# Seven half products in place of eight for the second MLP's first product, with the residual spilled there too

## The chip, the cores and the metric

The kernel runs on one core of a Trainium2 chip. The metric is the device time of one execution in microseconds (us); lower is better. Five engines work side by side, each on its own instruction queue: TensorE (PE in the profile; its weight loads are PEld), VectorE (DVE), ScalarE (ACT), GpSimd (POOL) and SyncE (SP), which here issues the DMAs.

## The reference

Two layers over 512 latent tokens and 256 context tokens with 1024 channels. Layer 0 mixes tokens by pooling, layer 1 by attention; each is followed by a squared-ReLU MLP with 4096 inner channels. In the second layer only the latent tokens go through the MLP.

```python
def sq_relu_mlp(h, w_in, w_out):
    return jnp.square(jax.nn.relu(h @ w_in)) @ w_out
...
        x = x + gt1 * rms_norm(y_lat, g_mix_post[i])
        m_lat = sq_relu_mlp(modulate(rms_norm(x, g_mlp_pre[i]), sh2, sc2), w_mlp_in[i], w_mlp_out[i])
        x = x + gt2 * rms_norm(m_lat, g_mlp_post[i])
```

Everything is float32. `h @ w_in` is called the first product below, the product with `w_out` the second.

## The kernel before

Each float32 operand of a product is kept as two parts, a high part rounded to the matmul's number format and a low part that holds the rest; a product is three matmuls, high x high, high x low, low x high. ScalarE makes the high part (a copy), VectorE the low part (a subtraction). This is what `split` (line 120 ff.) and `Ring.load` (line 129 by its helper) do with every weight tile that a DMA brings into one of three raw buffers.

An MLP (`mlp`) runs over 16 groups of 256 inner channels. For each group it loads 256 columns of `w_in` and 256 rows of `w_out`, computes the first product and its squared ReLU into `hid`, and then the second product for each tile of 128 tokens (`out_mm`, line 748), which `out_ev` (lines 757 to 761) adds to the accumulator `acc`. The second product of group g comes behind the first product of group g + 1. The last two groups' second products are put together, and the closing steps `last0` or `last1` (norm, gate, residual) are woven between their tiles.

The first MLP (layer 0, 768 tokens) and the second (layer 1, 512 tokens) differ in the first product.

- The second MLP uses `Inner` for all its groups: two blocks of 128 inner channels, each 8 slices of 128 channels times 3 parts, so 48 matmuls of 128 x 512 (line 535). `square` takes ReLU and square of each block. Its weights go through `ring1`, four buffers used in turn, two for `w_in` and two for `w_out`.
- The first MLP uses `Inner` for groups 0 and 1 only and `Seven` for groups 2 to 15. There tokens, channels and inner channels are each cut in half, and of the eight half products seven are computed, from sums of halves (the scheme of Strassen in Winograd's form): `chain` is one half product, 4 slices x 3 parts = 12 matmuls, here 384 tokens wide (line 648), and `run` chains the seven through four PSUM banks `a`, `b`, `c`, `e`. Between the products ScalarE copies a partial sum from bank to bank (lines 656 to 662) and VectorE folds two of them into SBUF (lines 664, 666).

Once per MLP `sums` computes the four sums of activation halves (S1 to S4, lines 593 to 596) from the float32 activations, which still lie in `acc`, the place of the second product's sum. The room for S1 to S4 is that of the residual `xr`, the gate and a scratch tile: the residual is written to DRAM (`spill`, line 572), the pool is closed, and another is opened in its place. For each group `weights_sums` computes the sums of weight halves (T1 to T4) and splits them (lines 614 to 631); their only place is `unit[1]` and the now unused quarter of the activations. The second product's weights have one place, `unit[2]`, refilled in two halves (lines 120, 121). Before the last stage `before0` closes the sums' pool, builds the gate anew (`gate_diag`, lines 305 to 311) and reads the residual back (line 1013).

In the second MLP the residual and the gate stay where they are. `extra1` computes the last gate's modulation on VectorE in four of the groups (`ada_sum`, lines 254 to 263) and its gate at group 10.

PSUM is used as two tiles of two banks (`psA`, for the first product) and four tiles of one bank (`psB`, for the second product, transposes and gates). The order of the instructions on each engine is made when the kernel is built: the framework's scheduler takes the program's order and moves instructions by simulated times (`schedule_with_timeline_sim=True`), some of them pinned with `keep_in_program_order`. So matmuls of the second product lie between those of the first.

Of the kernel before, what the change touches and what calls it, by code (L numbers as in the profile page):

```python
# [9 lines left out]
F32 = mybir.dt.float32  # L10
# [7 lines left out]
P = 128  # L18
D = 1024
KT = D // P  # L20
LAT = 512
# [32 lines left out]
def backbone(ctx: ExitStack, tc, x, c, ctx_in, c_ctx, w_ada, b_ada, g_mix_pre, g_mix_post,  # L54
# [11 lines left out]
    held = ExitStack()  # L66
# [6 lines left out]
    xr, gate, junk = residents(held)  # L73
# [489 lines left out]
    place_of = [(t % 2) * 3 + t // 2 for t in range(NT)]  # L563

    HN = TOK // 2
    quad = lambda z, u, h: [z[:, 4 * u + k, HN * h:HN * h + HN] for k in range(4)]
    A11, A12, A21, A22 = ((quad(hH, u, h), quad(hL, u, h)) for h in range(2) for u in range(2))
    S = {}

    def sums():  # L570
        for t in (4, 5, 0, 1, 2, 3):
            sy.dma_start(spill[:, t], xr[:, t])
        held.close()
        S["held"] = ExitStack()
        pool = S["held"].enter_context(tc.tile_pool(name="sums", bufs=1, side="right"))
        f, parts[0] = pool.tile([P, 8520], F32R, name="sums"), pool.tile([P, 192], F32, name="parts")
        u = unit[0]
        n4 = 4 * HN
        at = {1: (f[:, 0:n4], f[:, n4:2 * n4]), 2: (f[:, 2 * n4:3 * n4], f[:, 3 * n4:4 * n4]),
              4: (u[:, 0:n4], u[:, n4:2 * n4])}  # L580
        k4 = lambda z: [z[:, HN * k:HN * k + HN] for k in range(z.shape[-1] // HN)]
        for n, (hi, lo) in at.items():
            S[n] = k4(hi), k4(lo)
        h3, l3 = f[:, 4 * n4:5 * n4], [u[:, 2 * n4:2 * n4 + 2 * HN], f[:, 5 * n4:5 * n4 + 2 * HN]]
        S[3] = k4(h3), [z for x in l3 for z in k4(x)]
        src = acc.rearrange("p (q u k h n) -> p u h k q n", u=2, k=4, h=2, n=P)

        def put(n, j, a, b, op):
            hs = slice(2 * HN * j, 2 * HN * j + 2 * HN)
            wide = lambda z: z.rearrange("p (k q n) -> p k q n", k=2, n=P)  # L590
            w = work_tile()[:, 0:2 * HN]
            for m in range(2):
                ve.tensor_tensor(out=wide(w)[:, m], in0=a[:, m], in1=b[:, m], op=op)
            hi, lo = (h3[:, hs], l3[j]) if n == 3 else (z[:, hs] for z in at[n])
            sc.copy(hi, w)
            ve.tensor_tensor(out=lo, in0=w, in1=hi, op=ALU.subtract)
            return wide(w)

        for j in range(2):
            a11, a21, a12, a22 = (src[:, u, h, 2 * j:2 * j + 2] for u in range(2) for h in range(2))  # L600
            w1 = put(1, j, a21, a22, ALU.add)
            w2 = put(2, j, w1, a11, ALU.subtract)
            put(4, j, a12, w2, ALU.subtract)
            put(3, j, a11, a21, ALU.subtract)

    def weights_sums(g):
        raw = raw_load(w_mlp_in[0, :, g * 256:(g + 1) * 256].rearrange("(k p) n -> p k n", p=P), 256)
        rv = raw.rearrange("p (k h n) -> p h k n", h=2, n=P)
        b11, b12, b21, b22 = (rv[:, h, 4 * u:4 * u + 4] for u in range(2) for h in range(2))
        k4 = lambda z: z.rearrange("p (k n) -> p k n", n=P)  # L610

        def put(reg, src, n):
            hi, lo = reg[:, 0:n], reg[:, n:2 * n]
            sc.copy(k4(hi), src)  # L614
            ve.tensor_tensor(out=k4(lo), in0=src, in1=k4(hi), op=ALU.subtract)
            ops = lambda z: [[z[:, 512 * m + P * k:512 * m + P * k + P] for k in range(4)] for m in range(n // 512)]
            return list(zip(ops(hi), ops(lo)))

        B11, B21 = put(unit[1][:, 0:2048], rv[:, 0], 1024)
        tt = work_tile()  # L620
        t1, t2 = k4(tt[:, 0:512]), k4(tt[:, 512:1024])
        ve.tensor_tensor(out=t1, in0=b12, in1=b11, op=ALU.subtract)
        ve.tensor_tensor(out=t2, in0=b22, in1=t1, op=ALU.subtract)
        T1, T2 = put(unit[1][:, 2048:4096], k4(tt), 1024)
        tu = work_tile()
        ve.tensor_tensor(out=k4(tu[:, 0:512]), in0=b22, in1=b12, op=ALU.subtract)
        ve.tensor_tensor(out=k4(tu[:, 512:1024]), in0=b21, in1=t2, op=ALU.subtract)
        def put3(m0, nm, src):
            hi, lo = (z[:, 0:4, HN + P * m0:HN + P * (m0 + nm)].rearrange("p k (m n) -> p m k n", n=P) for z in (hH, hL))
            sc.copy(hi, src)  # L630
# [621 lines left out]
```

## Time and profile before

| | |
|---|---|
| time, median of 3 runs | 1220.46 us (1219.82 to 1220.71) |
| the profiled execution | 1220.63 us, its span 1218.7 us |
| TensorE busy | 1172.3 us, 96% of the span |
| VectorE busy | 903.3 us, 74% |
| ScalarE busy | 566.6 us, 46% |
| first MLP's groups 2 to 15 | about 150 to 580 us of the span |
| second MLP | from 852 us, steady from 916 us; last stage from 1190 us |

A row of a group of instructions gives line, engine, operation, output <- inputs, shape and count, then busy us and mean ns of one, then the idle time of the engine before them and what ended it. In the chain of waits a row gives start, length and what ran; the chain steps of a run of matmuls give their pace, since a single matmul's own duration (390 ns at 512 wide) overlaps its neighbours'. A busy TensorE is not one at its peak.

### The profile page before, as it was taken

How to read it: one execution, taken by the hardware profiler on the slowest of the kernel's cores; microseconds unless marked ns; L12 is line 12 of the kernel's file. 1: busy time of each engine (PE TensorE's matmuls, PEld its weight loads, DVE VectorE, ACT ScalarE, POOL GpSimd, SP SyncE). 2: the span in 40 equal slices, each digit the busy share in tenths (PEclk: the TensorE clock that was granted, in tenths of full speed). 3: DMA queues.
4: the chain of work that ended last, by engine and by line, in shares of the span. 5: the costliest groups of instructions: out<-in, count | busy, mean ns of one | idle time of the engine just before them, and what ended most of it. 6: DMA issues, size and time to landing. Idle time of an engine off the chain costs nothing.

```text
span 1218.7 us, 16348 instructions
## 1 busy us (share of the span) xinstructions
PE 1172.3 (96%) x6434; PEld 1016.1 (83%) x6434; DVE 903.3 (74%) x1494; ACT 566.6 (46%) x969; POOL 103.5 (8%) x135
## 2 busy tenths in 40 slices
PE   6799999999999999999989989999899999999997
PEld 5579899998899889988878879988778888888886
DVE  3888968889899979876777689853566775546555
ACT  5676445443355345445575468844442312223222
POOL 1061000000000000000451231001000000000001
PEclk9999999999999999999999989999999999999999
DMA  9994024444344344423323011030244443322301
GB/s 327 348 341 160 6 99 139 138 138 157 120 139 138 118 159 134 143 104 117 126 69 104 35 35 36 1 105 1 70 138 138 138 138 108 134 70 70 104 1 69
DMA packets 105003, 143.67 MB, mean 118 GB/s; under 512 B 2608, under 2 KB 88032, under 8 KB 104928
## 3 DMA queue, kind: packets, MB, share of 16 engines
q1 hardware_dynamic: 104928, 142.64, 35.3%
q8 instruction: 50, 0.82, 0.3%
q14 instruction: 25, 0.20, 0.1%
HBM read 137.39 MB, written 5.24 MB: 117 GB/s over the span
## 4 chain that ended last, share of the span: by engine, by line
PE 41%; DVE 3%; issue 3%; ACT 2%; POOL 2%; POOLq 0%; DVEq 0%; ACTq 0%
PE pso L748 14%; PE psin L535 14%; PE psy L1115 3%; PE po L1089 3%; PE pss L1050 2%; PE psq L876 2%; PE pspt L1075 1%; ACT junk L154 1%; DVE xr L319 1%; POOL rs L885 1%; DVE work L901 0%; POOL ms L165 0%; POOL rs L167 0%; PE psx L344 0%; DVE units L1078 0%
## 5 line engine op out<-in xcount | busy, mean ns | idle before, releaser
L748 PE MATMUL pso<-units,rb 128*128 128x512 f32 x1542 | 369.8, 391 | 2.3 <-DVE units L129 1.2
L748 PEld LDWEIGHTS pso<-units,rb 128*128 128x128 f32 x1542 | 288.1, 188 | 60.0 <-ACT units L120 1.9
L761 DVE TENSOR_TENSOR acc<-acc,pso 128x512 f32<-128x512 f32 x239 | 155.4, 681 | 91.4 <-PE pso L748 91.0
L259 DVE SCALAR_TENSOR_TENSOR rows<-raw,cond,rows 128x256 f32<-128x256 f32 x280 | 124.5, 483 | 1.0
L748 PE MATMUL pso<-ra,rb 128*128 128x512 f32 (+1 forms) x390 | 91.3, 386 | 0.0
L165 POOL TENSOR_SCALAR ms<-ss 128x1 f32<-128x1 f32 x21 | 11.1, 527 | 942.9 <-ACT junk L154 942.2
L535 PE MATMUL psin<-ra,units 128*128 128x512 f32 (+1 forms) x320 | 87.5, 373 | 0.1
L748 PEld LDWEIGHTS pso<-ra,rb 128*128 128x128 f32 x390 | 72.5, 188 | 15.1 <-ACT rb L550 0.4
L126 ACT CAST units<-raw 128x2048 fp32r<-128x2048 f32 (+1 forms) x29 | 40.3, 1417 | 93.6 <-PE pso L748 76.5
L535 PE MATMUL psin<-ra 128*128 128x512 f32 x256 | 80.5, 390 | 0.0
L126 ACT CAST ra<-raw 128x2048 fp32r<-128x2048 f32 x16 | 30.4, 1907 | 96.2 <-PE pso L748 68.4
L648 PE MATMUL psin<-ra,units 128*128 128x384 f32 x336 | 66.1, 339 | 0.7 <-ACT psin L660 0.6
L535 PEld LDWEIGHTS psin<-ra,units 128*128 128x128 f32 x320 | 58.6, 188 | 9.1 <-ACT work L544 0.3
L648 PE MATMUL psin<-sums,units 128*128 128x384 f32 x336 | 64.4, 339 | 1.5 <-ACT units L614 1.4
L648 PEld LDWEIGHTS psin<-ra,units 128*128 128x128 f32 x336 | 59.4, 188 | 4.2 <-ACT psin L660 0.9
L648 PEld LDWEIGHTS psin<-sums,units 128*128 128x128 f32 x336 | 59.2, 189 | 3.9 <-ACT units L614 2.2
L129 DVE TENSOR_TENSOR units<-raw,units 128x2048 fp32r<-128x2048 f32 (+1 forms) x27 | 47.8, 1796 | 18.8 <-ACT units L126 18.8
L535 PEld LDWEIGHTS psin<-ra 128*128 128x128 f32 x256 | 48.1, 188 | 10.0
L129 DVE TENSOR_TENSOR ra<-raw,ra 128x2048 fp32r<-128x2048 f32 x16 | 36.6, 2292 | 24.5 <-ACT ra L126 24.5
L740 ACT COPY pso<-acc 128x512 f32<-128x512 f32 x42 | 24.3, 589 | 65.2 <-DVE acc L761 65.2
L876 PE MATMUL psq<-units,ra 128*128 128x512 f32 x216 | 52.1, 392 | 0.0
L535 PE MATMUL psin<-rb,ra 128*128 128x512 f32 x128 | 49.9, 390 | 0.0
(221 smaller groups left out, 2145.5 us busy)
## 6 DMA issues: line engine op xcount, KB each, us to landing
raw<-in_w_ada SPq DMA_DIRECT2D x48, 1024.0 KB, 5.3
raw<-in_w_mlp_in SPq DMA_DIRECT2D x32, 1024.0 KB, 5.3
raw<-in_w_mlp_out SPq DMA_DIRECT2D x32, 1024.0 KB, 5.0
raw<-in_w_qkv SPq DMA_DIRECT2D x6, 1024.0 KB, 5.1
raw<-in_w_o SPq DMA_DIRECT2D x4, 1024.0 KB, 5.0
spill<-xr SPq DMA_DIRECT2D x6, 512.0 KB, 8.5
xr<-spill SPq DMA_DIRECT2D x6, 512.0 KB, 6.7
xr<-in_x SPq DMA_DIRECT2D x4, 512.0 KB, 4.3
```

What stands on the lines that cost most here:

```text
L126: a = gp.tensor_copy(hi, raw) if pool_hi else sc.copy(hi, raw)
L129: b = (gp if pool_lo else ve).tensor_tensor(out=lo, in0=raw, in1=hi, op=ALU.subtract)
L259: ve.scalar_tensor_tensor(out=r, in0=raw[:, k, :], scalar=cond[:, k, c:c + 1], in1=r, op0=ALU.mult, op1=ALU.add)
L535: te.matmul(ps[:, bank, o:o + ln], w[:, k, fs], rhs, start=(k == 0 and n == 0), stop=(k == KT - 1 and n == 2))
L648: te.matmul(bank, w[k], a[k], start=start and k == 0 and m == 0, stop=stop and k == 3 and m == 2, skip_group_check=True)
L740: sc.copy(ps, accv[:, t, c0:c0 + w])
L748: te.matmul(pss[h][:, 0:cols[h][1]], a[:, f, ts_], w[:, f, cols[h][0]:sum(cols[h])], start=(n == 0 and not seeded[t]), stop=(n == len(seq) ...
L761: ve.tensor_tensor(out=d, in0=d, in1=ps[:, 0:w], op=ALU.add)
L876: te.matmul(ps, a[:, k, sl], w[:, k % 4, :], start=(k == 0 and n == 0), stop=(k == KT - 1 and n == 2))
L1050: te.matmul(ps[:, c2, 0:384], a[:, sl], b[:, kv, 384 * c2:384 * c2 + 384], start=(n == 0), stop=(n == 2))
L1089: te.matmul(po[:, 0:256], v[:, kt, hs], p[:, kt, qs], start=(kt == 0 and n == 0), stop=(kt == NT - 1 and n == 2))
L1115: te.matmul(ps, a[:, k, sl], w[:, k % 4, o:o + width], start=(k == 0 and n == 0), stop=(k == KT - 1 and n == 2))
```

## The change

The second MLP's groups 2 to 15 compute their first product as seven half products too, 256 tokens wide. `sums` and `weights_sums` become the class `Halved`, made once for each MLP with its own places: the second MLP's weight sums lie in `ra[:, 4096:8192]`, its B22 in `rb[:, 2048:3072]`, T3 and T4 in the unused quarter of the activations, S1 to S4 all in the residual's room. The residual (four tiles) is spilled at the second MLP's start and read back before its last stage, and the gate, before at group 10, is built there (`restore`). `ring1` is not used any more: the output weights have `unit[2]` alone, and group 1's `w_in` is loaded ahead of group 0's `w_out`, not behind it. The tokens of a tile pair are placed so that each half is contiguous, as in the first MLP, and group 0's chunks and the ReLU follow that order (two ReLUs in place of one per block).

```diff
     def modulated_pair(t, i, s, hi, lo, works, wide, fine, on_act):
-        if (i, s) == (0, 1):
+        if s == 1:
...
     def chunks1(g):
         if g == 0:
-            return [[(0, 0, 0, 256)], [(1, 0, 256, 256)]], [(0, 2, 256, 0)]
+            return [[(0, 0, 0, None)], [(1, 0, 1, None)]], [(0, None, 0, 1), (1, None, 1, 2)]
...
+    class Halved:
+        def sums(self, order, held):
+            for t in order:
+                sy.dma_start(spill[:, t], xr[:, t])
+            held.close()
+            pool = self.held.enter_context(tc.tile_pool(name="sums", bufs=1, side="right"))
...
+            for j in range(2):
+                a11, a21, a12, a22 = (src[:, u, h, 2 * j:2 * j + 2] for u in range(2) for h in range(2))
+                w1 = put(1, j, a21, a22, ALU.add)
+                w2 = put(2, j, w1, a11, ALU.subtract)
+                put(4, j, a12, w2, ALU.subtract)
+                put(3, j, a11, a21, ALU.subtract)
+
+        def weights(self, g):
...
+            B11, B21 = put(self.bt[:, 0:2048], rv[:, 0], 1024)
+            tt = work_tile()
+            t1, t2 = k4(tt[:, 0:512]), k4(tt[:, 512:1024])
+            ve.tensor_tensor(out=t1, in0=b12, in1=b11, op=ALU.subtract)
+            ve.tensor_tensor(out=t2, in0=b22, in1=t1, op=ALU.subtract)
+            T1, T2 = put(self.bt[:, 2048:4096], k4(tt), 1024)
+            tu = work_tile()
+            ve.tensor_tensor(out=k4(tu[:, 0:512]), in0=b22, in1=b12, op=ALU.subtract)
+            ve.tensor_tensor(out=k4(tu[:, 512:1024]), in0=b21, in1=t2, op=ALU.subtract)
+            T3, T4 = put3(0, 2, tu.rearrange("p (m k n) -> p m k n", m=2, n=P))
+            B22, = put3(2, 1, b22.unsqueeze(1)) if self.b22 is None else put(self.b22, b22, 512)
+            S = self.S
+            return [(B11, self.A11), (T1, S[1]), (T2, S[2]), (B21, self.A12), (T3, S[3]), (B22, S[4]), (T4, self.A22)]
...
-    def mlp(i, inner, rg, hids, order, extra, mid, last, before_last):
+    def mlp(i, inner, own, home, hids, order, extra, mid, last, before_last):
-        if i == 0:
-            one = lambda z: Ring([z], True)
-            wi = w_in(i, 1, one(unit[1]))
-            for f in range(2):
+        one = lambda z: Ring([z], True)
+        wi = w_in(i, 1, one(unit[1]))
+        for f in range(2):
+            if len(inner.chunks) > 2 - i:
                 inner.part(len(inner.chunks) - 1, f)
-                inner.square(f)
-            wo_ = w_out(i, 0, one(unit[2]))
-            sums()
-        else:
-            wo_, wi = w_out(i, 0, rg, True), w_in(i, 1, rg, True)
...
+            inner.square(f)
+        wo_ = w_out(i, 0, one(home))
+        own.sums(order, held[i])
         for g in range(NG - 1):
-            if i == 0:
-                if g:
-                    wo_, products = w_out(i, g, one(unit[2])), weights_sums(g + 1)
-            elif g:
-                wo_, wi = w_out(i, g, rg, g < 2), w_in(i, g + 1, rg, g < 2)
+            if g:
+                wo_, products = w_out(i, g, one(home)), own.weights(g + 1)
...
-            if i == 0 and g:
-                inner = Seven(products, hids[(g + 1) % len(hids)])
+            if g:
+                inner = Seven(products, hids[(g + 1) % len(hids)], own)
...
+    def restore(own, stack, tiles):
+        nonlocal xr, gate, junk
+        own.held.close()
+        xr, gate, junk = residents(stack)
+        for ci in range(2 - own.i):
+            gate_diag(own.i, GT2, ci)
+        for t in tiles:
+            sy.dma_start(xr[:, t], spill[:, t])
...
+    own1 = Halved(1, LAT, h1H, h1L, ra[:, 4096:8192], rb[:, 2048:3072],
+                  lambda f: {n: (f[:, 2048 * n - 2048:2048 * n - 1024], f[:, 2048 * n - 1024:2048 * n]) for n in (1, 2, 3, 4)})
+
+    def before1():
+        restore(own1, ctx, range(NL))
...
     def extra1(g):
...
         if g == 10:
             ada_fin(1, GT2, parts[1], 1)
-            gate_diag(1, GT2, 0, 1)
...
-    mlp(1, first1[0], ring1, hids1, range(NL), extra1, lambda g: None, last1, lambda: None)
+    mlp(1, first1[0], own1, unit[2], hids1, range(NL), extra1, lambda g: None, last1, before1)
```

More of the change, by code (lines that the diff above doesn't have):

```diff
@@ L71, in residents @@
                 pool.tile([P, D], BF16, name="junk"))
-    xr, gate, junk = residents(held)
+    xr, gate, junk = residents(held[0])
     psA = ctx.enter_context(tc.tile_pool(name="psA", bufs=2, space=PSUM))
@@ L562, in backbone @@
     ring = Ring(unit)
[L563 to L630, printed above, removed]
-            ve.tensor_tensor(out=lo, in0=src, in1=hi, op=ALU.subtract)
-            return [tuple([z[:, m, k] for k in range(4)] for z in (hi, lo)) for m in range(nm)]
-        T3, T4 = put3(0, 2, tu.rearrange("p (m k n) -> p m k n", m=2, n=P))
-        B22, = put3(2, 1, b22.unsqueeze(1))
-        return [(B11, A11), (T1, S[1]), (T2, S[2]), (B21, A12), (T3, S[3]), (B22, S[4]), (T4, A22)]
@@ L657, in run @@
             self.chain(e, 1, True, True)
-            sc.copy(r1[:, 0:HN], e)
+            sc.copy(r1[:, 0:hn], e)
             self.chain(a, 2, False, False)
@@ L791, in mlp @@
             inner.run((lambda: mid(g)) if g < NG - 2 else None)
-            if g == NG - 2 and i == 0:
+            if g == NG - 2:
                 wo_ = w_out(i, NG - 1, one(unit[1]))
-            if g < NG - 2:
+            else:
                 for t in range(tiles):
```

85 lines of the change are left out of this document (59 added, 26 removed).

## The prediction

> **What bounds the kernel now.** I read the page first, then the chain of waits, then busy time by stretch, then the groups of VectorE.
>
> ```profile
> span 1218.7 us, 16348 instructions
> PE 1172.3 (96%) x6434; PEld 1016.1 (83%) x6434; DVE 903.3 (74%) x1494; ACT 566.6 (46%) x969; POOL 103.5 (8%) x135
> ```
>
> TensorE is busy 96% of the span. The chain (start, length, engine, output, line, count) shows at what pace:
>
> ```profile
> 740.27 2.15 PE po L1089 x18
> ...
> 910.96 5.44 PE pso L748 x24
> 916.40 10.88 PE psin L535 x48
> 927.28 5.44 PE pso L748 x24
> ...
> 1189.76 21.92 PE pso L748 x108
> ```
>
> A group of the second MLP is 48 matmuls of the first product (10.88 us) and 48 of the second (2 x 5.44): 21.76 us, and nothing but TensorE stands between. A 512-wide matmul costs 10.88/48 = 0.2267 us. The 18 of line 1089 are 256 wide, each with weights of its own, as the new half products will be: 2.15/18 = 0.1194 us.
>
> By stretch (start:end, length, then busy us of PE, PEld, DVE, ACT, POOL, then granted clock, DMA share, GB/s):
>
> ```profile
> 140.00:160.00 20.00, 18.38 (x78) 15.12 (x77) 18.66 (x31) 6.34 (x9) 0.00 (x0) 0.91 0.31 108
> 180.00:560.00 380.00, 378.95 (x1917) 339.04 (x1916) 333.15 (x617) 182.47 (x273) 0.00 (x0) 1.00 0.40 132
> 240.00:260.00 20.00, 20.00 (x103) 18.29 (x102) 19.41 (x37) 9.00 (x14) 0.00 (x0) 1.00 0.48 157
> 360.00:380.00 20.00, 20.00 (x101) 17.92 (x100) 19.72 (x35) 13.59 (x21) 0.00 (x0) 1.00 0.47 150
> 560.00:580.00 20.00, 19.36 (x109) 17.57 (x109) 12.61 (x15) 9.94 (x16) 0.00 (x0) 1.00 0.50 171
> 861.00:893.00 32.00, 30.14 (x149) 25.63 (x148) 18.95 (x25) 15.62 (x20) 0.00 (x0) 0.95 0.20 66
> 916.40:960.00 43.60, 43.60 (x195) 36.08 (x194) 31.18 (x46) 12.23 (x12) 0.00 (x0) 1.00 0.44 144
> 960.00:1047.80 87.80, 87.80 (x389) 72.72 (x388) 58.10 (x79) 24.25 (x24) 0.00 (x0) 1.00 0.40 132
> 1112.92:1189.76 76.84, 76.84 (x341) 63.65 (x340) 40.90 (x49) 18.93 (x19) 0.00 (x0) 1.00 0.13 42
> ```
>
> The first MLP (180 to 560) already runs the seven products, 384 wide: with VectorE at 333.15/380 = 88% TensorE lost 1.05 us. In the second MLP TensorE loses nothing, and VectorE has 47% spare (40.90 of 76.84), 28% while it also sums the gate's modulation (31.18 of 43.60). So each TensorE microsecond saved there shortens the run, until something else is late.
>
> **The saving.** In 14 groups 48 matmuls of 512 become 84 of 256: 10.88 us become 84 x 0.1194 = 10.03, so 0.85 a group and 14 x 0.85 = 11.9 us. The second product, groups 0 and 1 and all after the last group stay. Another stretch bounds the price:
>
> ```profile
> 846.29 5.87 PE L1115 MATMUL psy<-units,ra 128*128 128x256 f32 x47
> ...
> 852.00 0.28 PE L535 MATMUL psin<-ra,rb 128*128 128x256 f32 x1
> ...
> L463 PE MATMUL pspool<-rb,ra 128*128 128x256 f32 x144 | 20.2, 290 | 0.0
> L1089 PEld LDWEIGHTS po<-units,rb 128*128 128x128 f32 x288 | 35.6, 191 | 1.1 <-DVE units L1078 1.0 <-issue 0.2
> ```
>
> From 846.29 to 852.00 lie 47 starts, 0.1215 us each: the saving would be 9.4. I take 0.1194, since line 1089 has the shape of the new work and a fresh weight load (191 ns) before each matmul, hidden behind its neighbours. The break-even price is 10.88/84 = 0.1295.
>
> The Trainium skill speaks against it: TensorE: Matmul & The Clock Gate, section "Back-to-back issue gap", gives a sustained 131 ns for a 512-wide matmul with its weight load and 81 ns for a 128-wide one. An estimate from these puts a 256-wide one near 98, and 84 x 98 exceeds 48 x 131 by 1.9 us: 27 us slower in 14 groups. The two rows above, 227 and 119 ns, contradict it; the measured pace decides.
>
> **VectorE in a steady group.**
>
> ```profile
> L121 DVE TENSOR_TENSOR units<-raw,units 128x1024 fp32r<-128x1024 f32 x34 | 40.9, 1222 | 6.1 <-ACT units L120 6.0
> L129 DVE TENSOR_TENSOR ra<-raw,ra 128x2048 fp32r<-128x2048 f32 x16 | 36.6, 2292 | 24.5 <-ACT ra L126 24.5
> L552 DVE TENSOR_TENSOR rb<-work,rb 128x512 fp32r<-128x512 f32 x32 | 22.1, 691 | 5.0 <-ACT rb L550 3.1
> L622 DVE TENSOR_TENSOR work<-raw 128x512 f32<-128x512 f32 x14 | 9.6, 688 | 5.2 <-DMA raw<-in_w_mlp_in 5.1
> L631 DVE TENSOR_TENSOR ra<-work,ra 128x1024 fp32r<-128x1024 f32 x14 | 17.2, 1226 | 0.9 <-PE pso L748 0.9
> L936 DVE TENSOR_TENSOR rb<-psq,rb 128x256 fp32r<-128x256 f32 x6 | 2.5, 419 | 0.0
> ```
>
> Now a group uses 40.90/76.84 x 21.76 = 11.6 us. Gone: two 2048-wide low parts (2 x 2.29) and four 512-wide operations of the squares (4 x 0.69). Added: two 1024-wide low parts of the output weights (2 x 1.22); the weight sums and their low parts, 4 x 0.69 + 3 x 1.23 + 0.69 = 7.1; two folds of 256 and two low parts of 512, 2 x 0.42 + 2 x 0.69 = 2.2. That gives 11.6 - 4.6 - 2.8 + 2.4 + 7.1 + 2.2 = 15.9 of 20.9 us, 76%. Four groups also carry the modulation's sums, all within 916.4 to 1047.8: (31.18 + 58.10 - 131.4 x 40.90/76.84)/4 = 4.8 us each, so 20.7 of 20.9, 99%. The row 360 to 380 shows VectorE at 99% and the row 240 to 260 at 97%, both with TensorE never idle. At 97% these groups last 20.7/0.97 = 21.3, 0.4 longer: 4 x 0.4 = 1.7 with the rounding. For the rest I charge what the first MLP lost: 1.05/380 over 14 x 20.9 = 293 us, 0.8. Together +2.5; if less of VectorE can be used, the four groups grow (a rival below).
>
> Inside the seven products ScalarE and VectorE must empty a bank while TensorE runs one other product, 12 x 0.1194 = 1.43 us:
>
> ```profile
> L656 ACT COPY psin<-psin 128x384 f32<-128x384 f32 x14 | 6.6, 471 | 5.2 <-PE psin L648 5.0
> ...
> PE psin L648 <- ACT psin L660: 0.6, 1, 0.6
> PE psin L648 <- ACT units L614: 1.4, 2, 1.2
> PE pso L748 <- DVE units L129: 1.2, 1, 1.2
> ```
>
> The copy takes 0.47 us at 384, and in the first MLP TensorE waited for it once in 14 groups (0.6 us), under a cover of 12 384-wide products. At 256 the copy is shorter too. I charge nothing beyond the 0.8 above.
>
> **The start.** New work comes between the residual's last write and group 2: four spills of 512 KB, then eight sums, while TensorE runs group 1 (10.88) and group 0's second product (10.88).
>
> ```profile
> 855.62 1.29 DVE L319 SCALAR_TENSOR_TENSOR xr<-acc,rs,xr 128x1024 f32<-128x1024 f32 x1 [0.85 <-POOL rs L167]
> ...
> 868.76 0.37 SPq L106 DMA_DIRECT2D raw<-in_w_mlp_in  x1
> ...
> spill<-xr SPq DMA_DIRECT2D x6, 512.0 KB, 8.5
> xr<-spill SPq DMA_DIRECT2D x6, 512.0 KB, 6.7
> ```
>
> The last row of the residual is ready at 856.9 and its spill lands 8.5 us later, at 865.4. What queues behind the spills on SyncE is the weight load that SyncE issues now at 868.76, so it isn't held. On VectorE 32.00 - 18.95 = 13.0 us are free from 861 to 893. The sums take 8 x (2 x 0.42 + 0.69) = 12.2 and group 2's weights 7.1: 6.3 too many. But the last 3.3 of the weights (2 x 0.69 + 1.23 + 0.69) are wanted only by the fifth product, 4 x 1.43 = 5.7 us later, which leaves 3.0. The evictions of group 0 queue behind the sums, since they overwrite the sums' source, and TensorE's four banks wait for those. The first MLP paid for the same step in the row 140 to 160: 1.62 idle, and a clock of 0.91 for 20 us, 1.8 more, together 3.4. I take 3.4, less the 1.2 us wait for line 129, which stands there now (895) and goes: +2.2. The bounds are -1.2 (all hidden) and 6.3 - 1.2 = 5.1.
>
> The Trainium skill, same page, section "What's actually happening", has the clock halve only after an idle window of about 3.4 us. The row shows it falling with 1.62 us idle; by the rule the start would cost 0.4 and the time would be 1.8 lower.
>
> **The end.** The residual comes back from DRAM and the gate is built after the last sums are read, one product (1.43 us) before the final 21.92 us.
>
> ```profile
> 1197.80 1.29 DVE L316 TENSOR_TENSOR work<-acc,gate 128x512 f32<-128x512 f32 x2
> 1199.93 1.41 DVE L319 SCALAR_TENSOR_TENSOR xr<-work,rs,xr 128x512 f32<-128x512 f32 x2 [0.85 <-POOL rs L167]
> ```
>
> The gate is wanted 1197.80 - 1189.76 = 8.0 us into that stage, the residual 10.2. The reload (6.7) ends 5.3 in. The gate's four 512-wide matmuls were there before (group 10). They need two of the four banks that the second product uses; the first MLP did the same within 560 to 580 and TensorE was idle 0.6 there: +0.6, bounds 0 and 2.5 (the wait for one tile's eviction if the banks run out, 8.0 - 5.44).
>
> **Sum.** -11.9 + 2.5 + 2.2 + 0.6 = -6.6. The profiled execution took 1220.63 (span 1218.7), the median of the three runs is 1220.46, 0.2 less: 1220.6 - 6.6 = 1214.0. Best of this case: -11.9 - 1.2, 1207.5. Worst: -9.4 + 5.1 + 2.5 + 0.6 = -1.2, 1219.4.
>
> **Rivals.** (1) Slower: the single copies of weights. Before, four buffers alternate; after, the first product's sums have one place, refilled between the fourth product of one group and the first of the next, and the output weights one, refilled during the seven products. That leaves 3 x 1.43 + 10.88 = 15.2 us for the first of these. In the first MLP 12 matmuls of 384 take 2.1 us,
>
> ```profile
> 335.59 2.27 PE L648 MATMUL psin<-ra 128*128 128x384 f32 x12
> 337.69 2.24 PE L648 MATMUL psin<-ra,units 128*128 128x384 f32 x12
> ```
>
> from one start to the next, and there it has 3 x 2.1 + 72 x 0.2267 = 22.6. If each group meets once the 1.2 us wait for line 614 that the first MLP met at its start, that is 14 x 1.2 = 16.8: 1230.8. It decides from 6.6/14 = 0.5 us a group. For it: 7.1 + 5.5 of evictions (8 x 0.69) already fill most of 15.2 on VectorE. Against it: the wait came twice in 14 groups, and the fill isn't wanted all at once. 13%.
>
> (2) Slower: the half products cost the 20.2/144 = 0.140 us of line 463. 84 x 14 x (0.140 - 0.1295) = 12.3 slower, with 5.3 of the other terms: 1238.2. It decides at 0.1295. Line 463 is short runs with gaps between; the two uninterrupted stretches speak against it, 4%. The page cited on the issue gap says this too.
>
> (3) No change: VectorE can't be used above the first MLP's 88%. The four full groups then last 20.7/0.88 = 23.5, 2.6 each over 20.9 and 10.4 in all, in place of 1.7: 1222.7. The rows at 97 and 99% speak against it, 9%.
>
> **How the numbers follow.** My forecast has 74%, with its own range of 1207.5 to 1219.4. A measurement of this kernel tells apart 0.2%, 2.4 us, so faster ends at 1218.0 and no change at 1222.9: 2 of the 74 lie past 1218.0, and (3) lies just inside no change. Faster 0.72, same 0.02 + 0.09 = 0.11, slower 0.13 + 0.04 = 0.17. The range goes from the best case to (3), 1222.8; (1) and (2) stay outside.
>
> **What would show it.** Right: 84 matmuls of 256 a group with 12 of them near 1.43 us, a steady group near 20.9 us, VectorE near 76%, 97 to 99% in the four groups with the modulation, TensorE idle some 2 to 4 us around group 2. Wrong: a wait for the weights' or sums' producers that returns in every group; half products above 0.1295; a granted clock below 1.00 in steady groups; TensorE idle in the last stage.

## The result, and the profile after

The changed kernel takes 1222.88 us (median of 10 runs, 1220.25 to 1223.81), the kernel before 1220.49 (10 runs): a ratio of 1.0018, with an interval of 1.0008 to 1.0028. Forecast were 1214.0 and a range of 1207.5 to 1222.8. The change makes the kernel 0.2% slower where it was to save 0.5%. Labels e1 to e18 below (there is no e16) are the experiments' kernels; a line number in a row is that of the row's own kernel, a few lines apart from one kernel to the next. "After" is the changed kernel.

The page of after, the execution that took 1223.81:

```profile
span 1221.8 us, 17689 instructions
PE 1167.8 (96%) x6938; PEld 1030.8 (84%) x6938; DVE 966.6 (79%) x1633; ACT 627.4 (51%) x1122; POOL 105.3 (9%) x135
```

The chain of waits of after (start, length, engine, output, line, count):

```profile
910.47 1.43 PE psin L649 x12
...
979.29 1.06 ACT units L120
980.37 1.23 DVE units L121
982.32 1.20 DVE acc L763 x2
984.30 3.13 PE psin L649 x24
...
1006.39 3.13 PE psin L649 x24
...
1048.34 6.05 PE psin L649 x48
1054.39 5.47 PE pso L750 x24
...
1069.66 6.05 PE psin L649 x48
```

Twelve matmuls of a half product take 1.43 us, 0.1194 each: the price that was forecast. A group's matmuls alone are then 84 x 0.1194 + 48 x 0.2267 = 20.91 us. But a steady group takes 1069.66 - 1048.34 = 21.32, and a group with the gate's modulation 1006.39 - 984.30 = 22.09, longer than the 21.76 before. There the chain leaves TensorE: it goes through ScalarE's and VectorE's split of the output weights. VectorE's timeline at that place (after a row, idle time and what ended it):

```profile
980.37 1.23 DVE L121 TENSOR_TENSOR units<-raw,units 128x1024 fp32r<-128x1024 f32 x1 [0.45 <-ACT units L120]
981.51 0.48 DVE L259 SCALAR_TENSOR_TENSOR rows<-raw,cond,rows 128x256 f32<-128x256 f32 x1
981.91 0.41 DVE L666 TENSOR_TENSOR work<-work,psin 128x256 f32<-128x256 f32 x1
982.24 1.28 DVE L763 TENSOR_TENSOR acc<-acc,pso 128x512 f32<-128x512 f32 x2
983.43 0.48 DVE L259 SCALAR_TENSOR_TENSOR rows<-raw,cond,rows 128x256 f32<-128x256 f32 x1
983.83 0.42 DVE L668 TENSOR_TENSOR work<-work,psin 128x256 f32<-128x256 f32 x1
```

Line 666 is the fold that empties bank `a` for the seventh product. It takes 0.4 us, and it stands in VectorE's queue behind line 121, which waits for ScalarE's line 120, which waits for TensorE's own second product. TensorE's waits from 940 to 1060 (in all, times, longest):

```profile
PE psin L649 <- DVE work L666: 1.2, 4, 0.3
PE psin L649 <- DVE work L668: 0.9, 4, 0.2
```

That is the idle time, 2.1 us of the 4.7 that the four groups take over their matmuls. The distances between the matmuls' starts hold most of the rest at the same two places: at 982.38 the seventh product starts 0.47 us late and its second matmul another 0.1, at 984.30 the next group's first product 0.38 and 0.1.

Where the time went, from TensorE's timeline. To leave out what lies ahead of the change (TensorE reached it 1.4 us later in the profile of after), I count from the start of the attention output's last run of matmuls (846.29 before, 847.71 after) to group 1's first product, and from there to TensorE's end (e5 and e18 are kernels of the next section):

| us | before | after | e5 | e18 |
|---|---|---|---|---|
| to group 1's first product | 24.64 | 28.22 | 28.20 | 24.72 |
| from there to TensorE's end | 340.74 | 338.53 | 333.73 | 336.35 |
| sum | 365.38 | 366.75 | 361.93 | 361.07 |

The second row of after holds -11.9 for the matmuls, -1.4 up to 925 (mostly the wait of before at group 2, which is gone), +7.0 in the groups from there to 1150, and +4.1 in the last ones (each the time of TensorE beyond its matmuls at 0.2267 and 0.1194 us, against the same of before); together -2.2. The first row adds 3.6. Two entries hold some time at a lower granted clock: 24.64 about 1.5 us (864 to 867) and 333.73 about 1.6 (1180 to 1183), with 256-wide matmuls 0.213 us apart there in place of 0.12.

### The profile page after: what moved, and what is told of

It is laid out like the page before. It is cut to its first block, busy times and chain, and to the rows that moved or that the text cites. A ratio compares the mean times of both kernels' runs of the same rounds, so it can differ in the third digit from the quotient of the medians.

```text
span 1221.8 us, 17689 instructions
## 1 busy us (share of the span) xinstructions
PE 1167.8 (96%) x6938; PEld 1030.8 (84%) x6938; DVE 966.6 (79%) x1633; ACT 627.4 (51%) x1122; POOL 105.3 (9%) x135
## 4 chain that ended last, share of the span: by engine, by line
PE 36%; DVE 6%; ACT 3%; issue 3%; POOL 2%; DMA 1%; POOLq 0%; DVEq 0%; ACTq 0%
PE pso L750 13%; PE psin L649 10%; PE psy L1109 3%; PE po L1083 3%; PE pss L1044 2%; PE psq L867 2%; PE psin L535 1%; PE pspt L1069 1%; ACT junk L154 1%; DVE acc L763 1%; DVE units L121 1%; ACT units L120 1%; POOL rs L876 1%; DVE xr L319 1%; DMA raw<-in_w_mlp_in 0%
## 5 line engine op out<-in xcount | busy, mean ns | idle before, releaser
L750 PE MATMUL pso<-units,rb 128*128 128x512 f32 (+1 forms) x1932 | 462.7, 391 | 1.6 <-ACT units L120 1.1
L750 PEld LDWEIGHTS pso<-units,rb 128*128 128x128 f32 x1932 | 357.7, 189 | 72.0 <-ACT units L120 2.1
L120 ACT CAST units<-raw 128x1024 fp32r<-128x1024 f32 x68 | 70.0, 1048 | 71.0 <-PE pso L750 64.8
L649 PE MATMUL psin<-ra 128*128 128x256 f32 (+1 forms) x448 | 94.8, 308 | 4.3 <-DVE work L666 2.0
L121 DVE TENSOR_TENSOR units<-raw,units 128x1024 fp32r<-128x1024 f32 x68 | 82.0, 1219 | 17.3 <-ACT units L120 17.1
L649 PE MATMUL psin<-sums,ra 128*128 128x256 f32 (+1 forms) x588 | 95.4, 296 | 0.0
L649 PE MATMUL psin<-rb,ra 128*128 128x384 f32 (+1 forms) x364 | 88.3, 310 | 0.0
L649 PEld LDWEIGHTS psin<-sums,ra 128*128 128x128 f32 x588 | 85.4, 191 | 2.0
L649 PEld LDWEIGHTS psin<-rb,ra 128*128 128x128 f32 x364 | 66.6, 189 | 1.2
L649 PEld LDWEIGHTS psin<-ra,units 128*128 128x128 f32 x336 | 59.3, 188 | 4.4 <-DVE units L614 1.0
```

The costliest lines, as they stand in the source:

```text
L120: sc.copy(hi[:, z], raw[:, z])
L121: ve.tensor_tensor(out=lo[:, z], in0=raw[:, z], in1=hi[:, z], op=ALU.subtract)
L649: te.matmul(bank, w[k], a[k], start=start and k == 0 and m == 0, stop=stop and k == 3 and m == 2, skip_group_check=True)
L750: te.matmul(pss[h][:, 0:cols[h][1]], a[:, f, ts_], w[:, f, cols[h][0]:sum(cols[h])], start=(n == 0 and not seeded[t]), stop=(n == len(seq) ...
```

## The experiments

Four explanations were tried first. A: the start is longer because the change no longer pins the first splits, so that they stand ahead of the last tile's norm; B: its new work is what costs. C: the four long groups wait because the output weights have one place; D: VectorE is too full there.

**e1: the first splits in program order again.**

```diff
+            a = sc.copy(hi[:, z], raw[:, z])
+            b = ve.tensor_tensor(out=lo[:, z], in0=raw[:, z], in1=hi[:, z], op=ALU.subtract)
+            if pin:
+                tc.keep_in_program_order(a)
+                tc.keep_in_program_order(b)
...
-                sc.copy(k4(hi), src)                     # the weight sums' high parts
+                a = sc.copy(k4(hi), src)
+                if self.i == 1 and g == 2:
+                    tc.keep_in_program_order(a)
...
-        wi = w_in(i, 1, one(unit[1]))
+        wi = w_in(i, 1, one(unit[1]), i == 1)
...
-        wo_ = w_out(i, 0, one(home))
+        wo_ = w_out(i, 0, one(home), i == 1)
```

> Changed kernel, but group 1's w_in, group 0's w_out and the first part of group 2's weight sums keep their place in the program on ScalarE and VectorE, so that they stand behind the last token tiles' norm and not ahead of it. Theory A (at the start the time goes because these weight splits, and one of them waiting for its DMA, stand ahead of the last tile's norm in the in-order queues): group 1's first product starts 3 to 4 us earlier after the attention output's last matmul (19 us in place of 22.5), time 1219.4. Theory B (the start costs what the sums cost on VectorE, whatever the order): no change, 1222.9.

Measured: 1225.73, ratio 1.0038 (1.0025 to 1.0051), a time that neither theory gave. The start came down to 24.70, as before the change, and the rest went up to 345.03: 2.5 us are lost at 883 to 897, and 4.2 at 908 to 925, a wait of 2.27 us for the fold at 917 and behind it 3 us of matmuls 0.213 us apart. So the order of the splits does set the length of the start, as A has it, but the 3.5 us and 3 more are lost 10 to 50 us later, and the kernel is slower, not faster.

**e2: the modulation's sums left out.**

```diff
-        if 3 < g < 8:
-            ada_sum(1, GT2, g - 4, 1, parts[1][:, 8 * g - 32:8 * g - 24])
+        if g == 3:
+            ve.memset(parts[1], 0.01)
```

> Changed kernel without the four sums of the last gate's modulation in the second MLP (the gate's modulation is filled with a constant; that part of the computation is left out). If VectorE's load makes groups 5 to 8 long: they shrink from 22.09 to the 21.3 us of the others, 4 x 0.77 = 3.1 us, 1219.8. If those groups are long for another reason (weights or DMA), nothing changes: 1222.9. In both cases the other groups stay at 21.3, 0.4 over the 20.9 of matmuls alone.

Measured: 1218.85, ratio 0.9986 (0.9976 to 0.9996); the four groups fall to 21.32 each, like their neighbours. Their length comes from VectorE's extra work. Whether from its amount or from its place in the queue, this run doesn't tell.

**e3: two places for the output weights.** `home` becomes a ring of `unit[2]` and `ra[:, 0:4096]`.

> Changed kernel, with two places in turn for the second MLP's output weights (the second in the memory of the attention's output, free by then) in place of one. Theory C (the fold of the fifth product stands on VectorE behind the low part of the output weights, which waits for ScalarE's high part, which waits for the last matmul that reads the single place; the seventh product waits for the fold): groups 5 to 8 fall from 22.09 towards 21.0 and the others from 21.3 to 21.0, 4 x 1.1 + 10 x 0.3 = 7 us, 1215.5. Theory D (VectorE is simply full in groups 5 to 8): these stay at 22.1, 1222 to 1223.

Measured: 1227.89, ratio 1.0057 (1.0042 to 1.0073). The chain of e3:

```profile
988.41 3.13 PE psin L649 x24
...
1005.49 1.06 ACT ra L120
1006.57 1.22 DVE ra L121
1008.52 1.20 DVE acc L763 x2
1010.50 3.14 PE psin L649 x24
```

Still 22.09 a group. The split is now of weights wanted a whole group later, and it stands at the same place: the scheduler moves it up to the moment when its place comes free, in front of the fold. C falls for these groups. That e3 is 5 us slower than after has other causes in its profile: a wait of 2.32 us for the fold at 917, with slower matmuls behind it (4.1 us together), and a start that is 2.7 us longer. The end is 1.9 us shorter than in after, so there the second place does help.

**e4: e1 and e3 together.**

> Both edits of e1_pin and e3_homes. Theories A and C together: 1222.9 - 3.5 - 7 = 1212.4, less than before. B and D: 1222.9. If only A holds 1219.4, if only C 1215.9.

Measured: 1222.35, ratio 1.0011 (1.0002 to 1.0020); the four groups unchanged. The 2.5 us that e1 lost at 883 to 897 are gone with the second place (0.03). For the four groups that left D, and a new theory Q: not VectorE's load but the order of its queue.

**e5: the same work with the folds in front.** `issue_after` queues what is built inside it behind a given instruction on that engine, without a wait.

```diff
+        def behind(s):                                # s: a Seven built before
+            st = ExitStack()
+            if i and s:
+                st.enter_context(tc.issue_after(s.fold))
+            return st
...
-                wo_, products = w_out(i, g, one(home)), own.weights(g + 1)
+                with behind(sevens and sevens[-1]):
+                    wo_ = w_out(i, g, one(home))
+                products = own.weights(g + 1)
...
-            extra(g)
+            with behind(sevens and sevens[-1]):
+                extra(g)
```

The last output weights go behind the fold of the seven products before the last.

> The changed kernel (1222.9) with one difference: in the second MLP VectorE's low part of the output weights (line 121) and the gate's modulation sums (line 259) are queued behind the two folds of the seven products that were written before them. The work is the same. Theory Q (queue order: the fold that TensorE waits for stands behind line 121, which itself waits for ScalarE): the 0.77 us of each of the four groups with the modulation fall to about 0.15 (-2.5), and of the last groups' 0.98 + 0.73 at lines 666 and 672 about 1.2 goes: 1219.2. Theory V (VectorE is full in those groups, whatever the order): the wait only moves to the weights' low parts, 1222 to 1223.

Measured: 1216.89, ratio 0.9975 (0.9965 to 0.9985): 6 us less than after by the medians, 5.2 by the ratios. The chain of e5, and two stretches of it, a group with the modulation and one without (start:end, length, then busy us of PE, PEld, DVE, ACT, POOL, granted clock, DMA share, GB/s):

```profile
960.17 5.75 PE psin L649 x48
...
981.19 5.75 PE psin L649 x48
...
1044.25 5.75 PE psin L649 x48
1050.00 5.47 PE pso L750 x24
...
1065.27 5.75 PE psin L649 x48
```

```profile
965.92:986.94 21.02, 21.02 (x134) 19.08 (x133) 19.56 (x33) 9.94 (x17) 0.00 (x0) 1.00 0.46 153
1050.00:1071.02 21.02, 21.02 (x134) 19.08 (x133) 16.50 (x23) 10.29 (x17) 0.00 (x0) 1.00 0.30 103
```

Every group takes 21.02 us, with or without the modulation. VectorE is 93% busy in the first stretch (19.56 of 21.02), and TensorE never idles. The scheduler makes all the queues anew for every kernel; TensorE's order in a steady group (runs of 24, 19, 12, 5, 48, 24) is that of after, and in the four groups eight matmuls of the second product moved behind the third half product. Q is shown, D falls: the 6.7 us that TensorE of after spends beyond its matmuls from 925 to 1150 are 0.6 here.

**e11: the half of e5 that concerns line 121.** The modulation's sums stay free.

> Half of e5 (1216.9): only the low part of the output weights (line 121) is queued behind the folds; the gate's modulation sums stay free, as in the changed kernel. If line 121, with its wait for ScalarE, is what held the folds: within 1 us of e5, 1217 to 1218, and the four groups with the modulation within 0.2 us of 21.2. If the sums ahead of the fold hold it as well: 0.4 us or more in each of these groups, 1219 or more.

Measured: 1218.25, ratio 0.9979 (0.9969 to 0.9990), a quarter of a us above the 1217 to 1218 of the first case, and all groups at 21.02. Line 121, with its wait for ScalarE, is what held the folds; the sums only lengthened the queue that stood behind it, which is why leaving them out (e2) helped.

**e6, e7, e8: e4 with the order of e5, and with ScalarE's split queued too.** In e6 the output weights' low part goes behind the fold and ScalarE's line 120 behind the `Relu` that empties the last bank (line 672 of after), both of the seven products before the last, since there are two places; e7 also keeps five matmuls of the second product back behind the seventh product; e8 also spreads the modulation over eight groups, in half steps of 128 columns, and finishes it at group 13 in place of 10.

```diff
+                st.enter_context(tc.issue_after(s.relu))           # e6: ScalarE
...
+                with tc.issue_after(tail) if hold else ExitStack():  # e7: TensorE
+                    te.matmul(...)
```

> Kernel e4 (start in program order, two places for the output weights; 1222.4) with the order of e5 on VectorE, and the high part of the output weights queued behind the last evacuation of the seven products on ScalarE. Theory Q: the stall at 910 to 914 (2.1 + 1.6 us) and the 1.0 in each of the four groups go for the most part, 3 + 2.5, and some 0.7 at the end: 1216. Theory V: only the stall at 910, where VectorE isn't full, can go: 1219 to 1220 and the four groups stay at 22 us.

> Kernel e6 with the last five matmuls of each group's second product queued behind the seventh half product in place of ahead of it, so that they run while ScalarE empties the bank that the next group's first half product needs. If the 0.25 to 0.3 us that a block of 48 half products takes over its matmuls are this evacuation: 0.25 us in each of 13 groups less than e6, about 3 us (1213 by theory Q). If these five matmuls are needed as cover for the fold: a wait for line 666's fold of 0.5 us or more ahead of the seventh product in each group, and 3 us or more slower than e6.

> Kernel e7 with the gate's modulation summed in eight half steps of 128 columns in groups 4 to 11 in place of four of 256 in groups 4 to 7; nothing left out, 4.8 us of VectorE's work a group become about 2.6. Theory V: the four groups give back most of what leaving the sums out gave (4.0 us): 3 us less than e7. Theory Q: the order has given that back already, within 1 us of e7.

Measured: e6 1231.06 (ratio 1.0088, 1.0074 to 1.0102), e7 1223.87 (1.0023, 1.0013 to 1.0033), e8 1222.84 (1.0017, 1.0006 to 1.0028). e6 and e7 missed by far. ScalarE's timeline in e6, and TensorE's waits there from 940 to 1150:

```profile
1054.36 0.38 ACT L677 ACTIVATE work<-psin 128x256 f32<-128x256 f32 x1
1054.63 1.98 ACT L120 CAST ra<-raw 128x1024 fp32r<-128x1024 f32 x2
1056.52 0.63 ACT L681 ACTIVATE work<-work 128x512 f32<-128x512 f32 x1
1057.05 0.37 ACT L663 COPY psin<-psin 128x256 f32<-128x256 f32 x1
```

```profile
PE psin L654 <- ACT psin L663: 7.3, 10, 1.2
```

The same thing on the other engine: queued behind the `Relu`, the split (line 120) came to stand in front of the short copy from bank to bank (line 663) that the next group's product waits for. With the five matmuls in between (e7) that wait goes, 7.2 us less than e6, and a smaller one, 0.67 us at the seventh product of each group, stays. e8 takes 1.0 us less than e7, as Q has it.

**e9, e13, e17: the end.** e9 is e5 with the last output weights split at group 10. e13 splits them at group 8 and builds the gate at group 10, as before the change, in a free part of `acc`. e17 is e5 with that gate and with 12 matmuls of group 14's second product kept back behind group 15's sixth and seventh half product.

```diff
+    gate1 = acc[:, 4 * D:6 * D].rearrange("p (a n) -> p a n", a=2)          # e13, e17
...
+            gate = gate1                                                    # at group 10
+            gate_diag(1, GT2, 0)
...
+                with tc.issue_after(inner.tails[h]) if held and n < 6 else ExitStack():   # e17
+                    te.matmul(...)
```

> Kernel e5 with the last group's output weights loaded and split at group 10 (their place is free since group 1) in place of beside group 14's. In e5 the last groups lose 2.46 + 1.61 us, and four instances of line 121 in a row stand there on VectorE; with two of them gone I expect 1.0 to 1.5 us left: 1214.2. If something else holds the end (the gate, the residual's return): 1216 to 1217.

> Kernel e5 (1216.9) with the end relieved: the gate built at group 10, in a free part of the accumulator, as the kernel before the change did, and the last output weights loaded and split at group 8. In e5 the end loses 2.46 + 1.61 + 0.66; in e9, where only the output weights were early, 1.38 + 0.85 were left of the first two, and 5 to 6 us came up behind line 305 of the gate's diagonals. If the gate is what the end costs beside the splits: 1.4 + 0.9 left, so 2.5 less than e5: 1214.4. If the seven products of group 15 lose this because no second product lies between them: 1216 to 1217.

> Kernel e5 (1216.9) with the gate built at group 10 (as in e13) and the group 14 part of the second tile's second product (12 matmuls of 512) kept back: six behind the sixth half product of group 15, six behind the seventh. If the end's loss is that nothing lies between the last seven products: of e5's 2.46 + 1.61 + 0.66 the first stays (four low parts of the output weights in a row on VectorE), the others go, less 1.5 for building the gate at group 10: 1216.0. If the hand-offs between ScalarE and VectorE are longer than the cover: 1217 or more.

Measured: e9 1221.58 (ratio 1.0013, 1.0002 to 1.0023) and e13 1219.16 (0.9986, 0.9977 to 0.9995), two misses, e17 1217.55 (0.9966, 0.9953 to 0.9979). The expectations count three losses at e5's end, 2.46 + 1.61 + 0.66 us. The middle one is no wait: the matmuls behind the first wait lie 0.213 us apart for 3 us, at a lower granted clock. VectorE's queue there, TensorE's wait, and the stretch behind it (the clock after POOL's column); then what TensorE waits for in e9:

```profile
1172.17 3.49 DVE L121 TENSOR_TENSOR units<-raw,units 128x1024 fp32r<-128x1024 f32 x3
1178.97 0.39 PE L649 MATMUL psin<-ra 128*128 128x256 f32 x1 [2.09 <-ACT psin L662]
1179.00:1184.00 5.00, 5.00 (x29) 5.00 (x30) 2.88 (x4) 1.43 (x2) 0.00 (x0) 0.66 0.00 0
```

```profile
1184.54 0.39 PE L649 MATMUL psin<-ra 128*128 128x256 f32 x1 [0.58 <-DVE work L666]
1189.56 1.22 PE L310 MATMUL psg<-diag,onesr 128*128 128x512 f32 x2 [3.33 <-DVE diag L305]
```

In e5 four low parts of output weights, three of them in a row (3.49 us), stand ahead of the squares of group 14. e9 took two of the four away, and the wait of 2.09 shrank to 1.19, but one of 0.58 came for the fold of line 666, and the gate's diagonals fell behind other work on VectorE, and TensorE's queue stood for them with the second product behind it: a new wait of 3.33. In e9's profile (1224.54, 3 us above its median) 2.5 us at the lower clock follow it. With the gate away from there, the last stage's run on TensorE, in e13 and in e17:

```profile
1193.37 16.78 PE L750 MATMUL pso<-units,rb 128*128 128x512 f32 x84 [2.16 <-ACT rb L677]
```

```profile
1190.17 16.76 PE L756 MATMUL pso<-units,rb 128*128 128x512 f32 x84 [0.77 <-ACT rb L679]
```

In e13 all of group 14's second product that has its data runs ahead of the last half products, and TensorE waits 2.16 us for the squares of group 15. With some of it kept back, 0.77. So part of what the end costs is missing cover: ScalarE's and VectorE's hand-offs of the last seven products lie open there, which in every other group run under the next group's products. Beyond its matmuls after 1150 TensorE spends 3.6 us in e5 without the slow stretch, 3.5 in e13 and 3.1 in e17, so at most 0.6 is gained at the end. The gate at group 10 costs 1.5 us there (e13 and e17) and the early output weights 1.1 at group 8 (e13), which is more than the gain; the medians have the same order.

**e10, e12, e14, e15: the start.** e10 is e9 and e14 is e13 with the pins of e1; e12 is e10 with the modulation of e8; e15 is e14 with group 0's evictions on ScalarE.

```diff
-                    ve.tensor_copy(d, ps)
+                    (sc.copy if i else ve.tensor_copy)(d, ps)      # e15
```

> Kernel e9 with the splits at the start of the second MLP kept in program order, as in e1. Between 840 and 880 this took 3.2 us off TensorE's waits in e1 and e4, but a stall of 3 to 4 us followed at 908 to 917, at a fold behind the weights' low parts. If the order of e5 also does away with that stall: 3 us less than e9, 1211. If the stall stays, because there the low parts of group 3's weights (not queued behind the fold) hold it: within 1 us of e9.

> Kernel e10 with the gate's modulation in eight half steps (groups 4 to 11). By theory Q the four groups lose nothing any more once the folds are in front, so this is within 1 us of e10. If VectorE's load itself costs time: 2 us or more less than e10.

> Kernel e13 with the splits at the start kept in program order. In e10 that took the waits at 855 to 872 from 9.3 to 5.9 us and put 4.2 in their place at 883 to 912 (evictions of group 0 behind the sums, 2.3; the fold of group 3, 1.9). If the start's loss is the new work on VectorE and only its place can be chosen: within 1 us of e13. If the order alone is at fault: 3 us less.

> Kernel e14 with the evictions of group 0's second product (eight copies of 512) on ScalarE in place of VectorE, where they queue behind the sums. If this queue is what costs 2.3 us at 883 to 897: they go, and the fold at 912 comes earlier too: 2 to 4 us less than e14. If the sums themselves or group 2's weights are late: no change.

Measured: e10 1219.78 (ratio 1.0000, 0.9990 to 1.0009; 1.8 less than e9 where 3 were expected if the stall went, and part of it from another end), e12 1222.07 (1.0019, 1.0010 to 1.0027), e14 1218.61 (0.9989, 0.9979 to 1.0000), e15 1218.40 (0.9984, 0.9975 to 0.9994). From e9 to e10 the start shrinks from 28.39 to 24.72, by 3.7, and in the 50 us that follow TensorE spends 4.7 us beyond its matmuls in place of 0.35: 2.3 at 883 to 897, and 1.9 at the fold of group 3, at 917, which stands behind the low parts of the next group's weights. At 883 to 897 TensorE waits for ScalarE's splits (lines 120 and 616), not for group 0's evictions (line 764), for which no engine waits there in this profile. Line 616 stands behind line 120, and that waits until group 0's second product has left the single place of the output weights. TensorE, two rows of ScalarE, and VectorE of e10:

```profile
896.49 0.38 PE L654 MATMUL psin<-ra 128*128 128x256 f32 x1 [0.92 <-ACT ra L616]
```

```profile
893.50 1.99 ACT L120 CAST units<-raw 128x1024 fp32r<-128x1024 f32 x2 [3.73 <-PE pso L755]
895.40 1.04 ACT L616 CAST ra<-raw 128x1024 fp32r<-128x1024 f32 x1
```

```profile
914.35 1.23 DVE L619 TENSOR_TENSOR ra<-raw,ra 128x1024 fp32r<-128x1024 f32 x1
915.49 0.68 DVE L619 TENSOR_TENSOR rb<-raw,rb 128x512 fp32r<-128x512 f32 x1
916.31 1.22 DVE L619 TENSOR_TENSOR ra<-work,ra 128x1024 fp32r<-128x1024 f32 x1
917.46 0.41 DVE L671 TENSOR_TENSOR work<-work,psin 128x256 f32<-128x256 f32 x1
```

In e15 the losses at 883 to 897 are 1.2 us in place of 2.3, but its time is not told apart from e14's. So with one place for the output weights the order of the splits only decides where the time is lost. This fits B; that the cause is VectorE's new work, which has to be done somewhere between 850 and 917, is argued and not shown, and the part at 883 to 897 went with a second place (e4). e12 is slower than e10, though nothing of Q or D says so. Its profile shows two new waits for ScalarE (0.67 and 0.56) at 1108 to 1110, and 1.3 us of lower clock in the end's 7.6 us beyond the matmuls (e10 5.9); as in e8, the modulation is also finished later. Why it is slower stays open.

**e18: e17 with the start of e15.**

> Kernel e17 with the start of e15 (splits in program order, group 0's evictions on ScalarE). If start and end add up: as much less than e17 as e15 was less than e13 (0.8 us): 1215. If the start's gain is taken back later as in e1: within 0.3 us of e17 or above it.

Measured: 1215.84, ratio 0.9962 (0.9947 to 0.9976), the fastest by its median; its interval overlaps those of e17 and e5. By the ratio it saves 4.6 us against before, with all of the reference's work done. In the profiles start and end do not add up: against e17 the start is 3.65 us shorter (28.37 to 24.72) and the rest 3.3 longer (333.08 to 336.35).

## Why the prediction failed

**The saving (-11.9) was right.** 12 half products' matmuls take 1.43 us, and the break-even price of rival (2) was not met. The Trainium skill's TensorE: Matmul & The Clock Gate, section "Back-to-back issue gap", from which 98 ns were estimated, is contradicted once more: 119 ns here, with fresh weights for each.

**The step that failed is "VectorE in a steady group", the +2.5.** I worked out VectorE's load, 15.9 of 20.9 us and 20.7 in the four groups, and charged 0.06 us a steady group and 0.4 in each of the four. Measured were 0.41 and 1.18, together 7.0 by 1150. The load was no bad estimate (16.5 and 19.6 in e5), and it isn't what costs. What I did not ask is what stands in front of the fold in the queue. The first MLP's rate, 1.05 us in 14 groups, was carried over although its half products are half as long again (384 wide) and give the folds that much more time; that this is why the first MLP lost so little, no run tests. The prediction named the wait for a bank ("VectorE must empty a bank while TensorE runs one other product") and priced the operation (0.4 to 0.5 us) instead of the queue.

**The end (+0.6, bounds 0 and 2.5) was mis-sized: 4.1.** I followed the gate and the residual, and neither was late by much: TensorE waited 0.49 us for the gate in after. The seven products of groups 14 and 15 were not in the sum of the end at all. Before, TensorE ran from group 15's first product into the last stage without a wait; in after it waits 0.81 us for group 14's fold (line 666) behind low parts of weights, and 0.47 and 0.92 for ScalarE's lines 672 and 662 in group 15. With half products the last hand-offs lie open (e13, e17), and more low parts of weights stand in the queue there (e3, e5).

**The start (+2.2) came out right by luck, in another place.** 28.22 - 24.64 = 3.6, less the 1.4 of the old wait at group 2, is 2.1. The lower clock that I charged (1.8) isn't in after; it is in before (about 1.5, 864 to 867), so after's waits are some 5 us longer, not 3.6. In after the time is lost ahead of group 1, since the change drops two pins and the splits come ahead of tile 3's norm, which I did not price. ScalarE and VectorE of after there (line 154 opens the norm, line 319 writes the residual's last row, 5.7 us later than before, 4.3 without the 1.4 that lie ahead of the change):

```profile
854.85 2.93 ACT L120 CAST units<-raw 128x1024 fp32r<-128x1024 f32 x3
...
863.64 1.05 ACT L154 ACTIVATE junk<-xr 128x1024 bf16<-128x1024 f32 x1
```

```profile
855.92 3.50 DVE L121 TENSOR_TENSOR units<-raw,units 128x1024 fp32r<-128x1024 f32 x3 [0.60 <-ACT units L120]
...
861.32 1.29 DVE L319 SCALAR_TENSOR_TENSOR xr<-acc,rs,xr 128x1024 f32<-128x1024 f32 x1 [0.77 <-POOL rs L167]
```

The wait that I did describe, group 0's evictions behind the sums, shows neither in after, where TensorE loses nothing at group 2, nor where the pins are back: there it waits for ScalarE's splits at that place (e10, 2.3 us).

**The rivals.** (3), VectorE unusable above 88%, gave 1222.7, and 1222.88 was measured: the number was right and the mechanism wrong, as 93% without idle TensorE in e5 shows. (1), the single copies of weights, came closest in kind, since the refill of the single place does stand in the queue; but a second place changes nothing in the groups (e3). It takes 1.9 us off the end (e3) and, with the pins, 2.5 at 883 to 897 (e4 against e1). It decides from 0.5 us a group, and 0.4 to 1.2 were measured, from the order.

The sum by the measured terms: -11.9 + 7.0 + 2.1 + 4.1 = +1.3, against the 1.4 of the table above and +1.0 to +3.4 by the interval of the ratio.

## What to carry to other kernels

A step that shortens one engine's runs also shortens the cover under every hand-off between them. Ask of each short operation that the busy engine waits for what stands in front of it in its own engine's queue, and what that in turn waits for, before asking how full the engine is. Where a scheduler orders the queues by simulated times, bulk work that isn't urgent (here a weight split, e3) can drift to the moment when its buffer comes free, and a queue edge behind the urgent operation, which adds no wait of its own, was worth 5 to 6 us here (e5). Repairing one queue can put the same bulk in front of another engine's short operation, as e6 and e9 did, so look at the queues again after each repair.

## What the runs showed of the hardware

The granted clock was less regular than I took it to be. After and e13 have the same instructions at the second MLP's start, and in both TensorE waits 3.08 us for the same operation; TensorE in after, then a stretch of it with the clock after POOL's column, then both for e13:

```profile
866.58 1.53 PE L344 MATMUL psx<-ident,acc 128*128 128x128 f32 x12 [3.08 <-DVE acc L497]
```

```profile
866.00:876.00 10.00, 7.87 (x61) 7.22 (x61) 5.76 (x11) 5.46 (x12) 0.00 (x0) 1.00 0.04 13
```

```profile
863.03 2.82 PE L344 MATMUL psx<-ident,acc 128*128 128x128 f32 x12 [3.08 <-DVE acc L497]
```

```profile
866.00:876.00 10.00, 9.24 (x51) 8.66 (x52) 4.94 (x9) 4.50 (x11) 0.00 (x0) 0.70 0.01 2
```

The clock stayed at 1.00 in the one and was 0.70 in the other, whose twelve transposes took 2.82 us in place of 1.53 and whose start was 31.22 us long in place of 28.22. The Trainium skill's TensorE: Matmul & The Clock Gate, section "What's actually happening", has the clock halve after at least one idle window of about 3.4 us: after agrees, e13 doesn't, and in e5 a wait of 2.09 us was enough (0.66 from 1179 to 1184). In e1, e3, e4 and e5 one wait of 1.96 to 2.32 us was each time followed by 3 us of matmuls 0.213 us apart, which cost 1.4 to 1.6 us more; behind e13's 2.16 at 1193 there are none. A difference of 3 us between single profiles of such kernels can be this alone.
